# A hybrid decoder layer on one Trainium2 core: the first 128 tokens and the first 128 weight rows handled alone, the residual loaded in pieces

## Chip, core and metric

The kernel runs on one core of one Trainium2 chip. The metric is the device time of one execution in microseconds; three executions of the kernel before took 296.55, 297.00 and 297.28 us, so the median is 297.0 us. One further execution was profiled. All times inside it count from the start of its span.

## What is computed

One decoder layer over 512 tokens of width 1024, in f32:

```
h    = rms_norm(x, norm_w)                       # 512 x 1024
proj = h @ w_in                                  # 1024 x 4096, eight groups of 512 columns
hq, hf, hi, hg, aq, ak, av, ag = split(proj, 8)
o_h  = rms_norm(hgrn2(hq, hf, hi, lower_bound), hg_norm_w) * silu(hg)   # 4 heads, gated recurrence
o_a  = moba(rms(aq), rms(ak), av) * silu(ag)     # 8 heads, causal, blocks of 256 keys
out  = x + concat(o_h, o_a) @ w_out              # 1024 x 1024
```

## The kernel before

**Products.** Every product with a weight is made of three matmuls in the f32r format. Both factors are split in a high part (a cast) and a low part (the rest): the weights into `whi` (ScalarE, L109) and `wlo` (VectorE, one on GpSimd, L117), the turned and scaled x into `hTh` (ScalarE, L258) and `hTl` (VectorE, L266). One 128x512 result over 1024 rows takes 8 x 3 matmuls of 512 columns. The weights come in 40 tiles of 256 rows x 512 columns (512 KB); tile n is loaded by `load(n)`, cast by `split_hi(n)` and split by `split_lo(n)`. Group 0 (tiles 0 to 3) is the recurrent input, then seven more groups of the input projection, and 8 tiles of `w_out`.

**Turning x.** x is loaded in eight tiles: `x<i><h>` is 128 tokens (i = 0 to 3) by 512 columns (h = 0, 1), 256 KB. `x_turn(a, kp)` transposes two token tiles (a = 0: tokens 0 to 255; a = 1: 256 to 511) for the 256 columns of `kp`: four TensorE transposes into one PSUM tile, then two ScalarE evacuations of 256 columns that write `hTh`; `x_lo(a, kp)` writes `hTl` with two VectorE instructions.

**The opening.** The first stretch is written out by hand and all engines keep its order. The loads go to SP's queue in the order of `DSEQ`; the work follows the string `SEQ` (L128), word by word:

- `y7`: seven warm-up matmuls on a tile of ones (each is two instructions in the trace); `nt`: the norm weights are turned into a column;
- `t<a><kp>` and `l<a><kp>`: `x_turn` and `x_lo`; `wh<n>` and `wl<n>`: cast and split of weight tile n;
- `p<u><kp>`: for token tile u and weight tile kp the four matmuls that need only `whi`; `q<u><kp>`: the two with `wlo`;
- `sq<i>`: ScalarE's sum of squares of token tile i; `rs`: the root (VectorE, GpSimd); `rr`: the root as a row, copied over the partitions by DMA; `cv`, `cm`: small constants.

An engine works its words in this order and waits at the first one that is not ready. So TensorE's order is `y7 nt t00 t01 t10 t11 p00 q00 p10 q10 p30 q30 t03 p20 q20 t12 t02 p01 ...`, and ScalarE's is `t00 wh0 t01 sq0 t10 t11 wh1 t03 t12 t02 sq1 wh2 sq3 wh3 sq2 ...`. At the end of the string token tile by token tile gets its last products and `ev_i` evacuates it.

**The middle.** TensorE then runs through seven groups of 96 matmuls; the recurrence and the attention are threads whose steps a planner (`drive`, with the latencies in `LAT`) puts between these matmuls when the build expects their inputs to be ready. The planner's clock counts matmuls and transposes only.

**The output product.** `out_h` multiplies the recurrent half with the first four `w_out` tiles while the attention runs. Each of its eight results uses one of two PSUM tiles of the pool `pacc`. `out_fin` (L674 to L683) adds x to each result: at the first result of a column half it loads all four token tiles of x for this half in one DMA of 1 MB into `res` (L680), and VectorE adds the PSUM tile to it (L681). `res` lies in the buffer of `hTl`, so this load waits for the last matmul that reads `hTl`. `out_a` later adds the attention half and stores the result.

Of the kernel before, what the change touches and what calls it, by code (L numbers as in the profile page):

```python
# [8 lines left out]
F32 = mybir.dt.float32  # L9
F32R = mybir.dt.float32r  # L10
I32 = mybir.dt.int32
AF = mybir.ActivationFunctionType
ALU = mybir.AluOpType
# [8 lines left out]
def kernel(  # L22
# [12 lines left out]
    nc = tc.nc  # L35
    P = 128
    T, DM = x.shape[1], x.shape[2]
    NT = T // P
# [7 lines left out]
    xv = x[0].rearrange("(i p) c -> p i c", p=P)  # L46
# [4 lines left out]
    wpool = ctx.enter_context(tc.tile_pool(name="wpool", bufs=WB))  # L51
# [3 lines left out]
    ptr = ctx.enter_context(tc.tile_pool(name="ptr", bufs=2, space=bass.MemoryType.PSUM))  # L55
# [6 lines left out]
    xt = []  # L62
# [23 lines left out]
    W = {}  # L86
    raws = {}
    raw0 = []

    def load(n):  # L90
        if n < 0 or n >= len(stream):
            return
        src, c0, kp = stream[n]
        if n < WB:
            if n % 2 == 0:
                raw0.append(big.tile([P, 2, 2, 512], F32, tag=("f", "k", "q")[n // 2], name="raw0"))
            raw = raw0[n // 2][:, n % 2]
        else:
            raw = wpool.tile([P, 2, 512], F32, tag="raw", bufs=RB, name="raw")
        nc.sync.dma_start(  # L100
            out=raw,
            in_=src[kp * 256:(kp + 1) * 256, c0:c0 + 512].rearrange("(k p) c -> p k c", p=P))
        raws[n] = raw

    def split_hi(n):
# [15 lines left out]
    def split(n):  # L121
        if n < len(stream):
            split_hi(n)
            split_lo(n)

    POOL_LO = (3,)
    LAT = dict(lm=4.544, lev0=9.2567, lev=4.4882, copy=1.9908, rms=5.7036, silu=15.1764, qk=14.2881, soft=2.5598, softn=0.0041, acopy=4.5215, st=1.5748, ch=6.6909, DEPTH=2)
    SEQ = 'y7 nt t00 wh0 t01 sq0 t10 l00 t11 wl0 p00 q00 l01 wh1 p10 q10 l10 p30 q30 wl1 t03 l11 p20 q20 t12 t02 sq1 p01 q01 wh2 l03 l12 sq3 wh3 p21 q21 p11 q11 sq2 l02 p31 q31 wl2 p32 q32 rs wl3 p02 q02 p22 q22 cv t13 p12 q12 rr cm l13'  # L128
    DSEQ = 'x00 nw x10 w0 x20 x30 x01 x31 x11 w1 x21 w2 w4 v w3 w5'
    POOL_LO = (3,)  # L130
    for w in DSEQ.split():
        if w == "nw":
# [23 lines left out]
    hTh = big.tile([P, KT, T], F32R, tag="hTh", name="hTh")  # L156
    hTl = big.tile([P, KT, T], F32R, tag="hTl", name="hTl")
# [14 lines left out]
    def mm(o, a, b, start, stop, us):  # L172
        nc.tensor.matmul(o, a, b, start=start, stop=stop)  # L173
        clock[0] += us

    def tr(o, a):
        nc.tensor.transpose(o, a, ident)  # L177
        clock[0] += 0.109

    def spawn(gen, lat=0.0):  # L180
        threads.append([clock[0] + lat, (), gen, lat])
# [33 lines left out]
    X = {}  # L215
    rst = const.tile([P, NT], F32, name="rst")
    ssx = const.tile([P, NT], F32, name="ssx")
    nwc = const.tile([P, KT], F32, name="nwc")
# [29 lines left out]
    def x_turn(a, kp):  # L248
        wide = a == 0 and kp % 2 == 1
        tp = (psc if wide else ptr).tile([P, 512], F32, tag="sc" if wide else "tr", name="tp")  # L250
        X["tp", a, kp] = tp
        for d in range(2):
            kt = 2 * kp + d
            for i in range(2):
                tr(tp[:, (2 * d + i) * P:(2 * d + i + 1) * P], xt[2 * a + i][:, kt * P:(kt + 1) * P])
        for d in range(2):
            kt = 2 * kp + d
            nc.scalar.activation(hTh[:, kt, a * 256:a * 256 + 256], tp[:, d * 256:d * 256 + 256],  # L258
                                 AF.Copy, scale=nwc[:, kt:kt + 1])

    def x_lo(a, kp):
        tp = X["tp", a, kp]
        for d in range(2):
            kt = 2 * kp + d
            ts_ = slice(a * 256, a * 256 + 256)
            nc.vector.scalar_tensor_tensor(hTl[:, kt, ts_], tp[:, d * 256:d * 256 + 256], nwc[:, kt:kt + 1],  # L266
                                           hTh[:, kt, ts_].bitcast(F32), op0=ALU.mult, op1=ALU.subtract)


    def acc_tile(wide):  # L270
        return (psc if wide else pacc).tile([P, 512], F32, tag="sc" if wide else "acc", name="acc")
# [27 lines left out]
    k = big.tile([P, HH, T], F32, tag="k", name="k")  # L299

    def ev_i(u, ps):
        nc.scalar.activation(it[:, u, :], ps, AF.Copy, scale=rst[:, u:u + 1])
# [147 lines left out]
    def states():  # L450
        yield (LAT["st"], ("lev", 0), ("lev", 1))
        for n in range(NT - 1):
            cs = slice(n * P, (n + 1) * P)
            tp = ptr.tile([P, 512], F32, tag="tr", name="tp")
            for h in range(HH):
                tr(tp[:, h * P:(h + 1) * P], k[:, h, cs])
            kst = scratch()
            nc.scalar.copy(kst, tp)
            yield LAT["copy"]
            us = psc.tile([P, 512], F32, tag="sc", name="us")  # L460
            for h in range(HH):
                es = slice(h * DK, (h + 1) * DK)
                mm(us[:, es], kst[:, h * P:(h + 1) * P], it[:, n, es], True, True, 0.218)
            Sn = scratch()
            if n == 0:
                nc.vector.tensor_copy(Sn, us)
            else:
                for h in range(HH):
                    es = slice(h * DK, (h + 1) * DK)
                    m = (h % 2) * 4 + n  # L470
                    nc.vector.scalar_tensor_tensor(Sn[:, es], S[n][:, es], TL[h // 2][:, m:m + 1], us[:, es],
                                                   op0=ALU.mult, op1=ALU.add)
            S[n + 1] = Sn
            done[("S", n + 1)] = clock[0]
# [70 lines left out]
    A = {}  # L545
# [111 lines left out]
    res = {}  # L657
# [16 lines left out]
    def out_fin(part, hf, u, ps):  # L674
        cs = slice(hf * 512, hf * 512 + 512)
        if part == 0 and u == 0:
            if hf == 0:
                res["t"] = big.tile([P, 2, NT, 512], F32, tag="hTl", name="res")
            res[hf] = res["t"][:, hf]
            nc.sync.dma_start(out=res[hf], in_=xv[:, :, cs])  # L680
        nc.vector.tensor_tensor(res[hf][:, u, :], ps, res[hf][:, u, :], op=ALU.add)  # L681
        if part == 1:
            nc.sync.dma_start(out=ov[:, u, cs], in_=res[hf][:, u, :])  # L683
# [128 lines left out]
    with tc.manual_schedule(engines={mybir.EngineType.PE}):  # L812
        with tc.manual_schedule():
            accs = {}

            def part(u, kp, low):
                us = slice(u * P, (u + 1) * P)
                if u not in accs:
                    accs[u] = acc_tile(u >= 2)
                hi, lo = W[kp]  # L820
                for d in range(2):
                    kt = 2 * kp + d
                    wh, wl = hi[:, d, :], lo[:, d, :]
                    prods = ((hTh[:, kt, us], wl),) if low else ((hTh[:, kt, us], wh), (hTl[:, kt, us], wh))
                    for j, (a, b) in enumerate(prods):
                        mm(accs[u], a, b, kt == 0 and not low and j == 0, kt == KT - 1 and low, 0.216)

            def part_hi(u, kp):
                part(u, kp, False)

            def part_lo(u, kp):
                part(u, kp, True)

            acts = dict(cm=const_masks, cv=const_vec, sq=x_sq, rs=x_rstd, rr=x_rows, y=warm_up, nt=nw_col, t=x_turn, l=x_lo, p=part_hi, q=part_lo,
                        wh=split_hi, wl=split_lo)
            for w in SEQ.split():
                name = w.rstrip("0123456789")
                acts[name](*([int(w[1:])] if name == "y" else [int(ch) for ch in w[len(name):]]))
            for n in range(4, WB):
                split(n)  # L840
            for u in range(4):
                part_hi(u, 3)
                part_lo(u, 3)
                ev_i(u, accs[u])
            for kp in range(4):
                del W[kp]
                split(kp + WB)

        q2 = big.tile([P, 2, HH, T], F32, tag="q", name="q2")
        q = q2[:, 1]  # L850
        G = big.tile([P, NT, 512], F32, tag="G", name="G")
        gT = big.tile([P, NP, T], F32, tag="gT", name="gT")
        spawn(levels(0))
        spawn(levels(1))
        spawn(states())
        spawn(chunks())
        fa = fill_a()
        started = [False]

        def filler():  # L860
            yield from fa
            start_attention()
            wait_for(*[("read", n) for n in range(NT)])
            yield from out_h()

        drive(filler())
        for _ in out_a():
            pass
# [27 lines left out]
```

## Time and profile before

| | |
|---|---|
| three executions | 296.55, 297.00, 297.28 us |
| profiled execution | 297.17 us, of which the span between first and last instruction is 295.4 us |
| TensorE matmul busy | 287.6 us (97%) |
| VectorE, ScalarE, GpSimd busy | 175.0, 132.7, 57.1 us |
| DMA | 31.0 MB, 105 GB/s on average |

PE is TensorE's matmuls and transposes, PEld its weight loads, DVE VectorE, ACT ScalarE, POOL GpSimd, SP the engine that issues the DMAs. In a row of the timeline the first number is the start, the second the length (of the whole group, where it ends in a count such as x4), and what stands in brackets is the idle time just before it and what ended it. Matmuls overlap, so their lengths say less than the distance between their starts. In a row of a table by stretches the columns are: stretch, length, busy time of PE, PEld, DVE, ACT, POOL (with counts), granted TensorE clock, DMA share, GB/s.

### The profile page before, as it was taken

The page shows a single profiled execution, that of the slowest core. Times are in us where ns is not written, and L with a number is a line of the kernel's source. Part 1 is how long each engine was busy: PE and PEld are TensorE (multiplying, and loading weights), DVE is VectorE, ACT ScalarE, POOL GpSimd, SP SyncE. Part 2 cuts the span into 40 slices and gives each one's busy share as a digit, 9 for nine tenths or more (in the row PEclk, how much of TensorE's full clock was granted, in tenths as well). Part 3 has the DMA queues.
Part 4 walks back from the last instruction along what each step waited for, and adds up shares of the span by engine and source line. Part 5 has one row for each costly group of instructions (what it writes and reads, how often), then busy time and mean ns, then how long its engine had stood idle before and what let it go on. Part 6 is the DMA issues. An engine that isn't in the chain of part 4 may idle for free.

```text
span 295.4 us, 5115 instructions
## 1 busy us (share of the span) xinstructions
PE 287.6 (97%) x1945; PEld 236.7 (80%) x1945; DVE 175.0 (59%) x379; ACT 132.7 (45%) x248; POOL 57.1 (19%) x92
## 2 busy tenths in 40 slices
PE   7799999999999999999999999999999999999995
PEld 6588888888787777898888888888887787878884
DVE  3552653653699998357855785585384585653232
ACT  3754644420430475225511743753577676763000
POOL 1004201064000000010274223320004534330000
PEclk9999999999999999999999999999999999999999
DMA  6972375160260006100620099468287000000123
GB/s 189 352 282 104 15 106 201 43 242 0 73 213 4 2 2 227 60 0 0 215 73 0 8 261 208 95 168 207 47 229 279 0 2 0 2 2 2 71 101 112
DMA packets 21546, 31.00 MB, mean 105 GB/s; under 512 B 1413, under 2 KB 8338, under 8 KB 21522
## 3 DMA queue, kind: packets, MB, share of 16 engines
q1 hardware_dynamic: 21522, 30.68, 35.5%
q8 instruction: 15, 0.25, 0.3%
q14 instruction: 9, 0.07, 0.1%
HBM read 25.17 MB, written 2.10 MB: 92 GB/s over the span
## 4 chain that ended last, share of the span: by engine, by line
PE 93%; DMA 5%; SPq 1%; DVE 0%; issue 0%; DVEq 0%
PE acc L173 74%; PE tp L177 6%; PE ot L173 4%; PE sc L173 3%; PE pl L173 3%; DMA res<-in_x_dram 3%; DMA x<-in_x_dram 2%; PE ops L173 2%; PE us L173 1%; SPq L71 0%; DVE res L681 0%; SPq L100 0%; DVE res L717 0%; SPq L133 0%; PE tpv L778 0%
## 5 line engine op out<-in xcount | busy, mean ns | idle before, releaser
L173 PE MATMUL acc<-whi,hTh 128*128 128x512 f32 x160 | 65.3, 408 | 0.0
L173 PE MATMUL acc<-whi,hTl 128*128 128x512 f32 x160 | 63.0, 394 | 0.0
L173 PE MATMUL acc<-wlo,hTh 128*128 128x512 f32 x160 | 60.0, 391 | 0.0
L117 DVE TENSOR_TENSOR wlo<-raw,whi 128x1024 fp32r<-128x1024 f32 x39 | 47.1, 1230 | 12.1 <-ACT whi L109 11.6
L109 ACT CAST whi<-raw 128x1024 fp32r<-128x1024 f32 x40 | 41.5, 1048 | 13.4 <-DMA raw<-in_w_in_dram 6.3
L173 PE MATMUL acc<-hTh,whi 128*128 128x512 f32 x96 | 38.2, 397 | 0.0
L173 PE MATMUL acc<-hTh,wlo 128*128 128x512 f32 x96 | 37.5, 391 | 0.0
L173 PE MATMUL acc<-hTl,whi 128*128 128x512 f32 x96 | 37.4, 389 | 0.0
L163 POOL TENSOR_TENSOR r<-v,mh 128x8 f32<-128x8 f32 (+1 forms) x12 | 17.2, 1430 | 99.6 <-DVE v L161 99.5
L173 PEld LDWEIGHTS acc<-whi,hTl 128*128 128x128 f32 x160 | 30.3, 190 | 6.4
L173 PEld LDWEIGHTS acc<-whi,hTh 128*128 128x128 f32 x160 | 30.3, 190 | 6.3
L173 PEld LDWEIGHTS acc<-wlo,hTh 128*128 128x128 f32 x160 | 30.4, 190 | 5.9
L615 POOL TENSOR_SCALAR scr<-scr,rl 128x512 f32<-128x512 f32 (+3 forms) x32 | 17.0, 536 | 47.2 <-DVE rl L614 38.5
L173 PEld LDWEIGHTS acc<-hTh,wlo 128*128 128x128 f32 x96 | 18.0, 188 | 4.0 <-DVE wlo L117 0.2
L173 PEld LDWEIGHTS acc<-hTh,whi 128*128 128x128 f32 x96 | 18.0, 188 | 3.6
L173 PEld LDWEIGHTS acc<-hTl,whi 128*128 128x128 f32 x96 | 18.1, 188 | 3.5
L612 ACT ACTIVATE scr<-scr,nm 128x512 f32<-128x512 f32 (+3 forms) x32 | 17.7, 556 | 6.7 <-DVE nm L608 6.4
L173 PE MATMUL acc<-whi,mTa 128*128 128x512 f32 (+1 forms) x72 | 20.4, 367 | 0.0
L681 DVE TENSOR_TENSOR res<-acc,res 128x512 f32<-128x512 f32 x15 | 10.3, 689 | 15.7 <-PE acc L173 13.3
L177 PE MATMUL tp<-ident,scr 128*128 128x128 f32 x128 | 19.1, 275 | 0.0
L608 DVE CUSTOM_DVE_ANT_0 scr<-sc,bias 128x512 f32<-128x512 f32 (+3 forms) x32 | 14.6, 487 | 6.5 <-PE sc L173 6.2
L177 PEld LDWEIGHTS tp<-ident,scr 128*128 128x128 f32 x128 | 15.0, 140 | 4.0 <-issue 1.4
(138 smaller groups left out, 428.4 us busy)
## 6 DMA issues: line engine op xcount, KB each, us to landing
raw<-in_w_in_dram SPq DMA_DIRECT2D x32, 512.0 KB, 3.7
raw<-in_w_out_dram SPq DMA_DIRECT2D x8, 512.0 KB, 3.9
x<-in_x_dram SPq DMA_DIRECT2D x8, 256.0 KB, 6.4
res<-in_x_dram SPq DMA_DIRECT2D x2, 1024.0 KB, 9.1
out_dram<-res SPq DMA_DIRECT2D x7, 256.0 KB, 2.0
K<-K SPq DMA_DIRECT2D x8, 128.0 KB, 5.9
KL<-KL SPq DMA_DIRECT2D x8, 128.0 KB, 5.9
Q<-scr SPq DMA_DIRECT2D x8, 128.0 KB, 3.7
```

The source lines that it names most:

```text
L109: nc.scalar.copy(hi, raw)
L117: eng.tensor_sub(lo, raw, hi.bitcast(F32))
L163: nc.gpsimd.tensor_tensor(r, v, mh[:, 0:n], op=ALU.pow)
L173: nc.tensor.matmul(o, a, b, start=start, stop=stop)
L177: nc.tensor.transpose(o, a, ident)
L608: nc.vector.tensor_tensor_reduce(out=z[:, 0:n], in0=sc[:, 0:n], in1=bias[:, j, T - n:T], op0=ALU.add, op1=ALU.min, scale=1.0, scalar=3e38, ...
L612: nc.scalar.activation(z[:, 0:n], z[:, 0:n], AF.Exp, bias=nm, scale=-1.0, accum_out=l)
L615: nc.gpsimd.tensor_scalar(z[:, 0:n], z[:, 0:n], rl, 1.0, op0=ALU.mult, op1=ALU.mult)
L681: nc.vector.tensor_tensor(res[hf][:, u, :], ps, res[hf][:, u, :], op=ALU.add)
```

## The change

Three things are changed.

1. The first weight tile is loaded in two DMAs of 128 rows each, cast in two halves (`A0`, `B0`) and split in two halves (`a0`, `b0`). The order of the loads puts it ahead of x10, x20 and x30, and tile 1 ahead of the second column halves of x; tile 3 moves ahead of tile 4.
2. `t00`, the turn of tokens 0 to 255 for the first 256 columns, becomes `s00` and `s10`: one token tile each, two transposes, two evacuations of 128 columns (`x_turn1`), and their low parts `k00`, `k10` (`x_lo1`). The products of weight tile 0 become `P<u><kt>`: three matmuls for one token tile and 128 weight rows (`part1`). They are spread between the transposes, and the warm-up is cut in `y5` and `y3`. From `p32` on the string is the old one.
3. The residual is loaded in four DMAs of 256 KB per column half instead of one of 1 MB.

```diff
-        nc.sync.dma_start(
-            out=raw,
-            in_=src[kp * 256:(kp + 1) * 256, c0:c0 + 512].rearrange("(k p) c -> p k c", p=P))
+        rows = src[kp * 256:(kp + 1) * 256, c0:c0 + 512].rearrange("(k p) c -> p k c", p=P)
+        for ks in ((slice(0, 1), slice(1, 2)) if n == 0 else (slice(0, 2),)):
+            nc.sync.dma_start(out=raw[:, ks], in_=rows[:, ks])
...
-    SEQ = 'y7 nt t00 wh0 t01 sq0 t10 l00 t11 wl0 p00 q00 l01 wh1 p10 q10 l10 p30 q30 wl1 t03 l11 p20 q20 t12 t02 sq1 p01 q01 wh2 l03 l12 sq3 wh3 p21 q21 p11 q11 sq2 l02 p31 q31 wl2 p32 q32 rs wl3 p02 q02 p22 q22 cv t13 p12 q12 rr cm l13'
-    DSEQ = 'x00 nw x10 w0 x20 x30 x01 x31 x11 w1 x21 w2 w4 v w3 w5'
+    SEQ = 'y5 nt A0 y3 s00 a0 B0 k00 P00 b0 s10 P01 k10 P10 t10 P11 l10 wh1 t01 P20 P21 l01 wl1 t11 P30 P31 l11 p01 q01 sq0 t03 p11 q11 t12 t02 sq1 p21 q21 wh2 l03 l12 sq3 wh3 p31 q31 sq2 l02 wl2 p32 q32 rs wl3 p02 q02 p22 q22 cv t13 p12 q12 rr cm l13'
+    DSEQ = 'x00 nw w0 x10 x20 x30 w1 x01 x11 x31 x21 w2 w3 w4 v w5'
...
+    def x_turn1(i, kp):
+        tp = ptr.tile([P, 512], F32, tag="tr", name="tp")
+        X["tp1", i, kp] = tp
+        for d in range(2):
+            kt = 2 * kp + d
+            tr(tp[:, d * P:(d + 1) * P], xt[i][:, kt * P:(kt + 1) * P])
+        for d in range(2):
+            kt = 2 * kp + d
+            nc.scalar.activation(hTh[:, kt, i * P:(i + 1) * P], tp[:, d * P:(d + 1) * P],
+                                 AF.Copy, scale=nwc[:, kt:kt + 1])
...
-            nc.sync.dma_start(out=res[hf], in_=xv[:, :, cs])
+            for z in range(NT):
+                nc.sync.dma_start(out=res[hf][:, z, :], in_=xv[:, z, cs])
...
+            def part1(u, kt):
+                us = slice(u * P, (u + 1) * P)
+                if u not in accs:
+                    accs[u] = acc_tile(u >= 2)
+                hi, lo = W[kt // 2]
+                wh, wl = hi[:, kt % 2, :], lo[:, kt % 2, :]
+                for j, (a, b) in enumerate(((hTh[:, kt, us], wh), (hTh[:, kt, us], wl), (hTl[:, kt, us], wh))):
+                    mm(accs[u], a, b, kt == 0 and j == 0, False, 0.216)
+
+            def half_hi(d):
+                if d == 0:
+                    W[0] = tuple(wpool.tile([P, 2, 512], F32R, tag=t, name=t) for t in ("whi", "wlo"))
+                nc.scalar.copy(W[0][0][:, d], raws[0][:, d])
+
+            def half_lo(d):
+                hi, lo = W[0]
+                nc.vector.tensor_sub(lo[:, d], raws[0][:, d], hi[:, d].bitcast(F32))
```

## Rows read from the trace of the kernel before

**Rows 1.** Part 4 of the page: shares of the span, by engine, of the chain that ended last.

```profile
PE 93%; DMA 5%; SPq 1%; DVE 0%; issue 0%; DVEq 0%
```

**Rows 2.** The same chain in order of time: start, length, what. The pieces in it that are not TensorE's, and what follows the second.

```profile
2.96 6.96 DMA x<-in_x_dram
...
217.23 8.04 DMA res<-in_x_dram
225.36 0.70 DVE res L681
226.11 3.02 PE acc L173 x12
```

**Rows 3.** Timeline of PE in the opening: warm-up, transposes (tp), products (acc). The last two are the start of `p32` and of `q32`.

```profile
1.04 3.36 PE L241 MATMUL wp<-scr 128*128 128x128 f32 x14 [1.04 <-DVE warm L151]
5.63 1.76 PE L177 MATMUL tp<-ident,x 128*128 128x128 f32 x7 [0.63 <-DMA x<-in_x_dram]
...
8.96 0.45 PE L177 MATMUL tp<-ident,x 128*128 128x128 f32 x1 [1.57 <-DMA x<-in_x_dram]
9.96 1.75 PE L177 MATMUL tp<-ident,x 128*128 128x128 f32 x7 [0.55 <-DMA x<-in_x_dram]
11.36 0.77 PE L173 MATMUL acc<-whi,hTh 128*128 128x512 f32 x1
...
12.36 0.63 PE L173 MATMUL acc<-whi,hTh 128*128 128x512 f32 x1
12.79 0.63 PE L173 MATMUL acc<-whi,hTl 128*128 128x512 f32 x1
...
13.85 0.40 PE L173 MATMUL acc<-whi,hTh 128*128 128x512 f32 x1
...
18.43 1.03 PE L177 MATMUL tp<-ident,x 128*128 128x128 f32 x8
...
24.79 0.39 PE L173 MATMUL acc<-whi,hTh 128*128 128x512 f32 x1
...
25.69 0.61 PE L173 MATMUL acc<-wlo,hTh 128*128 128x512 f32 x2
```

**Rows 4.** Timeline of SP's queue in the opening: start and length of the issue of the loads.

```profile
8.03 1.20 SPq L100 DMA_DIRECT2D raw<-in_w_in_dram  x2
9.93 0.28 SPq L74 DMA_DIRECT2D vec<-in_hg_lb_logits_dram  x1
10.72 0.25 SPq L75 DMA_DIRECT2D vec<-in_hg_norm_w_dram  x1
11.40 0.22 SPq L77 DMA_DIRECT2D vec<-in_q_norm_w_dram  x1
12.08 0.22 SPq L78 DMA_DIRECT2D vec<-in_k_norm_w_dram  x1
13.44 0.22 SPq L77 DMA_DIRECT2D vec<-in_q_norm_w_dram  x1
```

**Rows 5.** Timeline of ACT: the cast of weight tile 0 and the first sum of squares, with what they waited for; `t12` and `t02`; `sq1`; `wh2`; two casts in a row.

```profile
8.03 1.04 ACT L109 CAST whi<-raw 128x1024 fp32r<-128x1024 f32 x1 [0.62 <-DMA raw<-in_w_in_dram]
...
10.79 1.06 ACT L223 ACTIVATE sq<-x 128x1024 f32<-128x1024 f32 x1 [0.97 <-DMA x<-in_x_dram]
...
19.06 1.57 ACT L258 ACTIVATE hTh<-tp,nwc 128x256 fp32r<-128x256 f32 x4 [0.98 <-PE tp L177]
20.51 1.07 ACT L223 ACTIVATE sq<-x 128x1024 f32<-128x1024 f32 x1
...
21.55 1.06 ACT L109 CAST whi<-raw 128x1024 fp32r<-128x1024 f32 x1
...
30.69 1.99 ACT L109 CAST whi<-raw 128x1024 fp32r<-128x1024 f32 x2
```

**Rows 6.** Timeline of DVE: two `x_lo` in a row and two splits in a row.

```profile
19.94 1.66 DVE L266 SCALAR_TENSOR_TENSOR hTl<-tp,nwc,hTh 128x256 fp32r<-128x256 f32 x4 [0.94 <-ACT hTh L258]
...
32.29 2.34 DVE L117 TENSOR_TENSOR wlo<-raw,whi 128x1024 fp32r<-128x1024 f32 x2
```

**Rows 7.** Timelines around the residual: SP's issues, VectorE's first addition, TensorE's first product after its wait.

```profile
214.05 3.09 SPq L100 DMA_DIRECT2D raw<-in_w_out_dram  x3
217.23 1.07 SPq L680 DMA_DIRECT2D res<-in_x_dram  x2
...
225.36 0.69 DVE L681 TENSOR_TENSOR res<-acc,res 128x512 f32<-128x512 f32 x1 [2.21 <-DMA res<-in_x_dram]
...
226.11 0.50 PE L173 MATMUL acc<-whi,mThh 128*128 128x512 f32 x1 [0.70 <-DVE res L681]
```

**Rows 8.** Busy time by stretches (columns as said above).

```profile
10.00:14.00 4.00, 4.00 (x14) 3.49 (x15) 2.00 (x5) 3.17 (x7) 0.00 (x0) 1.00 1.06 405
...
80.00:120.00 40.00, 40.00 (x617) 31.42 (x616) 37.48 (x71) 15.80 (x32) 0.00 (x0) 1.00 0.30 104
...
214.00:222.00 8.00, 8.00 (x38) 6.71 (x37) 6.28 (x14) 5.97 (x10) 0.65 (x1) 1.00 0.83 236
222.00:224.00 2.00, 2.00 (x16) 1.80 (x15) 0.33 (x2) 1.68 (x6) 1.87 (x4) 1.00 1.05 400
```

**Rows 9.** Timelines of POOL (the split of tile 3) and of PE (the first product that reads it, `wlo` of tile 3).

```profile
27.00 2.38 POOL L117 TENSOR_TENSOR wlo<-raw,whi 128x1024 fp32r<-128x1024 f32 x1
...
32.03 0.62 PE L173 MATMUL acc<-wlo,hTh 128*128 128x512 f32 x2
```

More of the change, by code (lines that the diff above doesn't have):

```diff
@@ L259, in x_turn, with x_lo1 @@
                                  AF.Copy, scale=nwc[:, kt:kt + 1])
+    def x_turn1(i, kp):
[8 more added lines that the diff above has]
+                                 AF.Copy, scale=nwc[:, kt:kt + 1])
+    def x_lo1(i, kp):
+        tp = X["tp1", i, kp]
+        for d in range(2):
+            kt = 2 * kp + d
+            ts_ = slice(i * P, (i + 1) * P)
+            nc.vector.scalar_tensor_tensor(hTl[:, kt, ts_], tp[:, d * P:(d + 1) * P], nwc[:, kt:kt + 1],
+                                           hTh[:, kt, ts_].bitcast(F32), op0=ALU.mult, op1=ALU.subtract)
     def x_lo(a, kp):
@@ L834 @@
             acts = dict(cm=const_masks, cv=const_vec, sq=x_sq, rs=x_rstd, rr=x_rows, y=warm_up, nt=nw_col, t=x_turn, l=x_lo, p=part_hi, q=part_lo,
-                        wh=split_hi, wl=split_lo)
+                        wh=split_hi, wl=split_lo, s=x_turn1, k=x_lo1, P=part1,
+                        A=half_hi, B=lambda _: half_hi(1), a=half_lo, b=lambda _: half_lo(1))
             for w in SEQ.split():
```

## The prediction, made before the result was known

> **What bounds the kernel now.** I read the chain that ended last first: 93% of it is TensorE [rows 1]. So the useful number of matmuls, which the change leaves alone, sets the time, and something is to be had only where TensorE stands still or runs slowly. The chain in order of time then shows two such places: 6.96 us behind the loads of x at the start, and 8.04 us in which the load of the residual stands in the chain, with an addition of 0.70 us behind it [rows 2]. The change touches both.
>
> The timeline of PE in the opening is to show three things [rows 3]. The first product starts at 11.36, after idle times that loads of x ended (0.63, 1.57 and 0.55 us). Products start 0.43 us apart (12.36, 12.79): 512 columns in 0.43 us is the 1.2 GHz level. From 24.79 to 25.69 four take 0.90 us, 0.23 us each, which is 2.4 GHz; the step lies just ahead of 13.85. The granted clock says 1.00 throughout this stretch [rows 8], so here the spacing tells the level, not that column. Ahead of the step PE had been without a pause since 9.96.
>
> **When the loads land.** SP starts load number n+8 when number n has landed: number 11 starts at 8.03, when the cast of weight tile 0 (number 3) starts [rows 4, 5]; number 13 at 9.93 is x30, which PE takes at 9.96 [rows 3, 4]; number 14 at 10.72 is x01, which ScalarE squares at 10.79 [rows 4, 5]. By that x10 lands at 5.6, w0 8.0, x20 8.9, x30 9.9, x01 10.7, x31 11.4, x11 12.1, w1 13.4. Landing follows the order of issue, so I put the new order on the same curve of bytes: w0's first half at 5.6 (x10's place), its second 6.8 (halfway to 8.0), x10 8.0, x20 8.9 and x30 9.9 as before, w1 11.4, all x by 14.1. Nothing later than w1 comes near a deadline.
>
> **The opening, step by step.** Durations of instructions that stand in a row behind one another: evacuation of a pair of 256 columns 0.73 (four in 1.57, then the sum of squares at 20.51), cast 0.94 (two in 1.99, one in 1.05), sum of squares 1.04 [rows 5]; `x_lo` 0.83, split 1.11 [rows 6]. Per 128 columns that is 0.095 on ScalarE (0.94 against 0.37 for 768 columns less) and 0.12 on VectorE, so the halves cost: cast 0.56, evacuations 0.54, split 0.64, `k` 0.60. None of them stands in the trace. As bounds I take half of the whole and the whole; between these the first products move by about 0.5 us either way. Each result is usable 0.1 us after its slot, and PE's transposes reach ScalarE 0.17 us after the next could start.
>
> `s00` is through on PE at 5.7 (warm-up 0.24 per instruction, transposes 0.22 [rows 3]). ScalarE has `A0` ahead of it, until 6.2, then the evacuations until 6.7. `P00` starts at 6.8 instead of 11.36, and its third product waits for `a0` and `k00` (VectorE to 7.74) and ends at 8.3. x10 has landed by then. At 0.43 each, `s10` ends at 8.8, `P01` at 10.0.
>
> The clock comes next. PE now runs nearly without pause from 6.8, 3.2 us before the 9.96 of the old order. I move the step by the same 3.2 us, from 13.4 to 10.2. Bounds: 8.4 (as soon as the gaps of `P00` end) and 13.4 (no earlier than before). The Trainium skill ("TensorE: Matmul & The Clock Gate", Part 1) says that this moment differs from run to run of one kernel, because what watches the activity doesn't start with the kernel; one profiled run cannot show it, and by that rule every moment between these bounds has to be allowed for.
>
> With 10.2: `P10` ends at 10.9, `t10` (x30 is there at 9.9) 11.4, `P11` 12.1, `t01` 12.5. `P20` waits 0.4 us for `l10` (evacuation to 12.4, VectorE 0.83) and ends at 13.6. Then 0.23 per product and 0.115 per transpose: `P21` 14.3, `t11`, `P30`, `P31` 16.1, `p01`, `q01` 17.5, `t03` 17.9, `p11`, `q11` 19.3, `t12` 19.8, `t02` 20.2, twelve products 22.96.
>
> Here a new wait appears. In the old order 24 products stand between `t02` and `p32`, now 12. ScalarE still has two pairs of evacuations, `sq1` and `wh2` between: 19.77 + 0.17 + 0.73 + 0.73 + 1.04 + 0.94 + 0.1 = 23.5. `p32` therefore waits 0.56 us; four products end at 24.4; `wlo` of tile 2 is ready at 23.5 + 1.11 + 0.15 = 24.8, so `q32` waits another 0.34 and starts at 24.77. Before it started at 25.69 [rows 3]; counted the same way the old order gives 25.7. The gain of the opening is 0.92 us. With the clock at 8.4 it is 1.4, at 13.4 it is -0.1. Behind the waiting `p32` and `q32` PE has only the old order, which the threads take up unchanged. What is late next is `wlo` of tile 3 on POOL: ready 2.65 us before its product (29.38 against 32.03 [rows 9]). After the change the cast of tile 2 ends 0.9 us later than before (23.5 against 22.6 [rows 5]) and this split with it, while the product comes 0.92 earlier: 0.8 us are left. It doesn't bind.
>
> That the gain reaches the end: the planner's clock counts the same matmuls and transposes, so PE's order behind stays. Where VectorE is nearly full (37.5 of 40 us, with PE at 40 of 40 [rows 8]) it works on evacuations that come earlier with PE.
>
> **The additional DMA issues** (one for w0, six for the residual) cost SP some 0.3 to 0.6 us each by the neighbouring rows [rows 4, 7]. They lie beside transfers: at 217 three weight tiles are still on their way, and no load but the residual stands behind them on SP.
>
> **The residual.** From 214 to 222 the core moved 8 x 236 GB/s = 1.89 MB [rows 8]; 1.57 MB of it are the three weight tiles issued just ahead [rows 7]. So at 222 the first 0.26 MB piece is through, and at 400 GB/s [rows 8] one more follows each 0.66 us. The whole half is through at about 223.8 and was seen as landed at 225.36, 1.5 us later; the first piece would then count at about 223.3, and its addition (0.69) end at 224.0. PE needs that PSUM tile at 225.41 (226.11 less 0.70 [rows 7]). The wait of 0.70 us goes. Bounds: nothing (the pieces land together) and 0.75. What is late next is the second piece, half a microsecond behind the first, and VectorE, which stood 2.21 us and gets its attention work done earlier. The Trainium skill ("DMA: Bandwidth & Descriptors", Rules for kernel authors) asks for at least 1 MiB per DMA; here x31 and x11, of 256 KB, land 0.68 us apart and w1, of 512 KB, 1.36 us after x11 [rows 4], the same 385 GB/s, so in a full queue the trace does not bear the rule out. By it each piece would come later, and the residual would give nothing.
>
> **Sum.** 0.92 + 0.70 = 1.62 us. The profiled execution took 297.17 us, a span of 295.4 and 1.8 around it; it becomes 295.55, span 293.8. It stands 0.17 above the median of 297.0, so the median becomes 295.4.
>
> **Rivals.**
> - *The clock steps no earlier* (13.4): the opening gives nothing, every product until then pays 0.20 us and only fills the former wait; the residual remains: 296.3. For it: pauses at 7.3 to 7.9 and the half-speed transposes between the products; against it: PE's pauses are shorter than before. The same time results if a later stage swallows the opening's gain; [rows 8] speak against that.
> - *The pieces land no earlier*: the opening alone, 296.1. Against it: loads land in order of issue.
> - *Slower: the halves of w0 are slow.* w0 took 2.4 us for 512 KB (5.6 to 8.0), the slowest load of the opening. If each half took as long as the whole did, w0's halves land at 6.8 and 9.2, x10 at 10.4 and all others 2.3 us later. The same steps (`P00` from 8.0, wait for x10 from 9.3 to 10.4, clock step later by the 0.44 us that 10.4 is behind 9.96) put `q32` at 27.5, 1.8 us late; less 0.70 that is +1.1: 298.1. It decides for slower when the loads behind w0 come about 2 us late; from 1 us on the opening gives nothing. Against it: the same bytes are in the queue, and 256 KB pieces cost no more elsewhere.
>
> **Chances.** Forecast 0.60, clock or loss later 0.22, pieces 0.10, slow halves 0.08. About 0.3% (0.9 us) is what a measurement of this kernel can tell from no change: faster means under 296.1. The forecast's own spread (0.92 between 0.4 and 1.4) keeps nearly all of it faster, 0.56, and half of the pieces' case and a little of the clock's add 0.08: faster 0.64, same 0.27, slower 0.09. Range: down to 297.0 - 1.4 - 0.75 less 0.6 for the opening's unmeasured halves and the spread of the times (0.7 over three), 294.2; up to 297.0, which takes in both mild rivals.
>
> **What would show it.** First product near 6.8 and products 0.23 us apart from about 10; an idle PE ahead of `p32`, ended by ScalarE's cast of tile 2, and ahead of `q32`, ended by VectorE; `q32` at 24.8; no idle PE at 225, and the first addition no later than 224 on the new scale. The prediction is wrong if products keep 0.43 us beyond 12, if x10 lands after 9, or if more than 0.3 us of PE's idle time appears between 32 and 215.

## The result, and the profile after

The changed kernel took 300.34 us (median of four executions, 299.82 to 301.13) against 297.14 for the kernel before beside it: a ratio of 1.013, 95% interval 1.008 to 1.018. Run once more in a later batch it took 299.00 against 296.66: 1.008, interval 1.005 to 1.011. So the change made the kernel about 1% slower; 295.4 was forecast. A ratio here and below is estimated from the single executions, without those more than 1.5% above the fastest of the same kernel, so it is not the quotient of the two medians. The profiled execution took 300.61 us, with a span of 298.8 against 295.4. The difference of 3.4 us lies in the two places that the change touches.

**The opening loses 2.3 us.** Timeline of PE in the kernel after, the rows that answer to [rows 3]; the last three are the start of `p32`, the start of `q32` and the turn of the root of the norm (`rp`), which started at 30.99 before and now starts at 33.30.

```profile
5.12 0.45 PE L177 MATMUL tp<-ident,x 128*128 128x128 f32 x2
7.34 0.50 PE L173 MATMUL acc<-whi,hTh 128*128 128x512 f32 x1 [1.78 <-ACT hTh L269]
7.80 0.50 PE L173 MATMUL acc<-wlo,hTh 128*128 128x512 f32 x1
9.80 0.79 PE L173 MATMUL acc<-whi,hTl 128*128 128x512 f32 x1 [1.49 <-DVE hTl L277]
10.39 0.63 PE L177 MATMUL tp<-ident,x 128*128 128x128 f32 x2
...
12.10 0.63 PE L173 MATMUL acc<-whi,hTh 128*128 128x512 f32 x1
12.52 0.63 PE L173 MATMUL acc<-wlo,hTh 128*128 128x512 f32 x1
...
14.65 0.63 PE L173 MATMUL acc<-wlo,hTh 128*128 128x512 f32 x1
...
26.60 0.50 PE L173 MATMUL acc<-whi,hTh 128*128 128x512 f32 x1 [0.45 <-ACT whi L109]
...
27.86 0.73 PE L173 MATMUL acc<-wlo,hTh 128*128 128x512 f32 x2
...
33.30 0.27 PE L232 MATMUL rp<-ident,rst 128*4 128x128 f32 x1
```

The first product comes four microseconds earlier than before, at 7.34. Then two things go wrong. The third product of `P00` waits 1.49 us for the low part of x, `hTl`. And from this product on they are 0.43 us apart until 15, where the old order was at 0.23 from 13.85. The same in the table by stretches, where the third number from the right is the granted clock:

```profile
7.00:8.00 1.00, 0.66 (x2) 0.37 (x2) 0.94 (x5) 1.00 (x4) 0.00 (x0) 1.00 0.89 344
8.00:9.00 1.00, 0.30 (x1) 0.00 (x0) 1.00 (x13) 0.06 (x1) 0.00 (x0) 0.83 1.05 365
9.00:10.00 1.00, 0.20 (x1) 0.20 (x1) 0.96 (x7) 0.00 (x0) 0.00 (x0) 0.50 0.99 309
...
14.00:15.00 1.00, 1.00 (x5) 0.89 (x4) 0.00 (x0) 0.53 (x2) 0.00 (x0) 0.50 1.05 399
15.00:16.00 1.00, 1.00 (x7) 0.71 (x6) 0.66 (x2) 1.00 (x2) 0.00 (x0) 0.75 0.79 290
```

Here the column tells the level too: 0.50 of 2.4 GHz is 1.2 GHz, from 9 to 15. It also tells that the clock had been up before: 0.83 between 8 and 9 means that it fell near 8.7, in the wait behind the second product. The lengths agree: two transposes at 5.12 took 0.45 us and two at 10.39 took 0.63; the first product behind a pause took 0.50 at 7.34 and 0.79 at 9.80. So the opening did not stay at the low level; it was at the high one when `P00` began and lost it in its pauses. VectorE's timeline says what `hTl` stood behind:

```profile
7.06 0.69 DVE L864 TENSOR_TENSOR wlo<-raw,whi 128x512 fp32r<-128x512 f32 x1 [3.11 <-ACT whi L860]
7.67 0.18 DVE L768 TENSOR_TENSOR gt<-ccol,s 128x32 int32<-128x32 int32 x1
...
9.30 0.18 DVE L783 TENSOR_SCALAR lmask<-part 128x32 int32<-128x32 int32 x1
9.40 0.60 DVE L277 SCALAR_TENSOR_TENSOR hTl<-tp,nwc,hTh 128x128 fp32r<-128x128 f32 x2
```

From 7.67 to 9.48 VectorE makes the masks of the recurrence (`const_tri`, L757 to L783), which nobody needs yet. They are no word of the string, and the build places them; that all engines keep the order of the opening holds for its words alone. In the old kernel they filled VectorE's idle time from 4.7 to 6.5, as the first and the last of those placed there show in its timeline:

```profile
4.72 0.18 DVE L748 TENSOR_TENSOR gt<-ccol,s 128x32 int32<-128x32 int32 x1
...
6.35 0.18 DVE L763 TENSOR_SCALAR lmask<-part 128x32 int32<-128x32 int32 x1
```

Now they stand between `a0` and `k00`.

**The middle** moves as one piece. The residual's load was issued at 217.23 [rows 7] and is issued at 219.49 now, 2.26 us later.

**The residual loses another 1.1 us.** Timelines of SP, VectorE, GpSimd and TensorE in the kernel after, answering to [rows 7]:

```profile
219.49 6.11 SPq L700 DMA_DIRECT2D res<-in_x_dram  x8
...
224.01 0.16 DVE L633 RECIPROCAL rl<-l 128x1 f32<-128x1 f32 x1 [0.54 <-ACT scr L631]
226.74 0.69 DVE L701 TENSOR_TENSOR res<-acc,res 128x512 f32<-128x512 f32 x1 [2.57 <-DMA res<-in_x_dram]
227.35 0.21 DVE L633 RECIPROCAL rl<-l 128x1 f32<-128x1 f32 x2
...
227.60 1.15 POOL L634 TENSOR_SCALAR scr<-scr,rl 128x384 f32<-128x384 f32 x2 [2.56 <-DVE rl L633]
...
228.24 1.11 PE L177 MATMUL tp<-ident,scr 128*128 128x128 f32 x6 [1.84 <-POOL scr L634]
```

Before, VectorE had four reciprocals of the attention (`rl`) and then the first addition; the last two of the four in the timeline of the kernel before:

```profile
222.39 0.16 DVE L614 RECIPROCAL rl<-l 128x1 f32<-128x1 f32 x1 [0.44 <-ACT scr L612]
222.99 0.16 DVE L614 RECIPROCAL rl<-l 128x1 f32<-128x1 f32 x1 [0.43 <-ACT scr L612]
```

Now it has two reciprocals, the addition, and the other two. The addition waits 2.57 us for its piece of x, and the reciprocals behind it, GpSimd's scaling and TensorE's transposes wait with it: 1.84 us of idle TensorE in place of the 0.70 of before [rows 7]. The first piece counted as landed 7.25 us after its issue, the whole half before 8.13 after.

### The profile page after: what moved, and what is told of

The parts are those of the page before. It is cut to its first block, busy times and chain, and to the rows that moved or that the text cites. A ratio compares the mean times of both kernels' runs of the same rounds, so it can differ in the third digit from the quotient of the medians.

```text
span 298.8 us, 5138 instructions
## 1 busy us (share of the span) xinstructions
PE 288.8 (97%) x1947; PEld 236.7 (79%) x1947; DVE 176.8 (59%) x382; ACT 132.9 (44%) x251; POOL 57.0 (19%) x92
## 4 chain that ended last, share of the span: by engine, by line
PE 91%; DMA 4%; DVE 2%; ACT 1%; issue 0%; SPq 0%; POOL 0%; ACTq 0%; DVEq 0%
PE acc L173 72%; PE tp L177 7%; PE ot L173 3%; PE sc L173 3%; PE pl L173 3%; DMA res<-in_x_dram 2%; PE ops L173 2%; DMA raw<-in_w_in_dram 2%; PE us L173 1%; DVE wlo L117 0%; ACT sq L223 0%; ACT hTh L258 0%; ACT whi L109 0%; DVE wlo L864 0%; ACT whi L860 0%
## 5 line engine op out<-in xcount | busy, mean ns | idle before, releaser
L173 PE MATMUL acc<-whi,hTh 128*128 128x512 f32 x160 | 66.1, 413 | 2.2 <-ACT hTh L269 1.8
L173 PE MATMUL acc<-wlo,hTh 128*128 128x512 f32 x160 | 61.4, 396 | 0.1
L117 DVE TENSOR_TENSOR wlo<-raw,whi 128x1024 fp32r<-128x1024 f32 x38 | 45.7, 1226 | 8.9 <-ACT whi L109 8.4
L109 ACT CAST whi<-raw 128x1024 fp32r<-128x1024 f32 x39 | 40.5, 1048 | 14.1 <-DMA raw<-in_w_in_dram 6.9
```

The source lines that it names most:

```text
L109: nc.scalar.copy(hi, raw)
L117: eng.tensor_sub(lo, raw, hi.bitcast(F32))
```

## Experiments

Twelve runs in three batches, each batch beside the kernel before; the last four ran on another chip than the first eight, so runs of different batches are compared by their ratios. Four theories stood at first: A, the masks ahead of `k00` cost the opening its gain; B, the finer order itself is slow, by the low clock; C, the pieces cost time because an addition got ahead of two reciprocals; D, the pieces cost nothing. All medians first, then what each says. Each run has twelve executions, the changed kernel again seven. The ratio is that to the kernel before in the same batch.

| run | median us (range) | before | ratio, 95% interval |
|---|---|---|---|
| changed, masks early | 298.49 (297.23 to 300.47) | 297.08 | 1.0043, 1.0013 to 1.0074 |
| changed, one load | 298.05 (296.39 to 298.95) | 297.08 | 1.0037, 1.0011 to 1.0063 |
| before, with pieces | 296.97 (295.65 to 299.12) | 297.08 | 1.0023, 0.9992 to 1.0054 |
| masks early, one load | 297.39 (296.16 to 298.34) | 297.08 | 1.0025, 0.9998 to 1.0051 |
| changed, again | 299.00 (298.14 to 301.22) | 296.66 | 1.0082, 1.0050 to 1.0114 |
| masks early, one load, cast first | 297.45 (296.11 to 297.74) | 296.66 | 1.0012, 0.9988 to 1.0037 |
| the same, pause filled | 295.40 (294.98 to 295.79) | 296.66 | 0.9966, 0.9947 to 0.9984 |
| masks early, pieces reversed | 296.94 (296.00 to 297.77) | 296.66 | 1.0007, 0.9985 to 1.0029 |
| before, pause filled | 295.33 (294.18 to 296.80) | 296.21 | 0.9976, 0.9951 to 1.0000 |
| masks early, reversed, filled | 294.97 (294.78 to 295.62) | 296.21 | 0.9956, 0.9932 to 0.9980 |
| changed, pause filled | 296.53 (295.70 to 298.52) | 296.21 | 1.0007, 0.9980 to 1.0033 |
| all four | 294.66 (294.47 to 295.00) | 296.21 | 0.9946, 0.9925 to 0.9967 |

**Masks early.** `const_tri` becomes a word of the string (`ct`), right behind `nt`.

```diff
-y5 nt A0 y3 s00 a0 B0 k00 P00
+y5 nt ct A0 y3 s00 a0 B0 k00 P00
```

> The changed kernel, with the 21 mask instructions of const_tri written into the opening's order right behind nt, where VectorE is idle, instead of being put by the build behind a0 and ahead of k00. Theory A (the loss of the opening comes from these instructions standing ahead of k00): k00 starts near 7.8 instead of 9.4, the third product of P00 near 8.4 instead of 9.8, the clock step comes as much earlier (about 14), and the time falls by 1.4 us to about 298.9. Theory B (the finer order itself is slow: halves, few products between waits, a low clock): P00 starts earlier, but PE waits elsewhere before the clock step, and the time stays within 0.5 us of the changed kernel's 300.3.

298.49: A, in part. The third product of `P00` starts at 8.48 instead of 9.80, `rp` at 30.84 instead of 33.30; the rest of these 2.46 us comes with the clock, which rose again at 11.7 in this execution and at 15.5 in the one above. By the ratios to before (1.0043 against 1.0082) this is worth 0.39%, 1.2 us, but the two intervals overlap, and the pair with one load in the same batch (298.05 and 297.39) gives 0.7. Nor are the masks out of the way. Written out as one word they run from 3.86 to 7.39 and now hold up `a0`, which the second product needs. Its timelines of VectorE and TensorE:

```profile
7.21 0.18 DVE L783 TENSOR_SCALAR lmask<-part 128x32 int32<-128x32 int32 x1
7.30 0.69 DVE L863 TENSOR_TENSOR wlo<-raw,whi 128x512 fp32r<-128x512 f32 x1
...
8.05 0.64 PE L173 MATMUL acc<-wlo,hTh 128*128 128x512 f32 x1 [1.18 <-DVE wlo L863]
```

In all seven profiles with the masks early this product starts at 8.05 or 8.06. No run has the masks behind `k00`. The residual stays bad, and this profile shows what an idle TensorE costs there beyond its own length. Its timeline of PE, then its table by stretches:

```profile
226.14 1.47 PE L177 MATMUL tp<-ident,scr 128*128 128x128 f32 x6 [2.18 <-POOL scr L634]
```

```profile
226.00:228.00 2.00, 1.85 (x10) 1.61 (x10) 1.10 (x8) 1.52 (x6) 1.13 (x4) 0.68 0.54 206
228.00:230.00 2.00, 2.00 (x7) 1.61 (x7) 0.89 (x6) 1.23 (x5) 1.53 (x4) 0.50 0.08 23
230.00:232.00 2.00, 2.00 (x11) 1.62 (x10) 0.00 (x0) 0.00 (x0) 0.93 (x2) 0.97 0.00 0
```

Behind a pause of 2.18 us TensorE was granted half its clock from about 226.7 to 230. The profiles of the pieces alone (2.41 us) and of the changed kernel again (2.35) show the same fall; in the execution above, with 1.84 us, the granted clock stayed at 1.00.

**One load per half of the residual.**

```diff
-            for z in range(NT):
-                nc.sync.dma_start(out=res[hf][:, z, :], in_=xv[:, z, cs])
+            nc.sync.dma_start(out=res[hf], in_=xv[:, :, cs])
```

> The changed kernel with the residual in one load per column half, as before. Theory C (the pieces made the build put the first addition ahead of two reciprocals on VectorE, and GpSimd and TensorE wait behind it): the four reciprocals stand ahead of the addition again, PE's idle time there is 0.7 us instead of 1.84, the time falls by 1.1 us to about 299.2. Theory D (the pieces cost nothing or help a little, the whole loss lies in the opening): the time stays at 300.3 or rises by up to 0.7.

298.05: C. By the ratios (1.0037 against 1.0082) it is worth 0.45%, 1.3 us, where 1.1 was expected, though these intervals too overlap a little. VectorE has its four reciprocals first again, and TensorE's idle time there is 0.27 us.

**The pieces alone, on the kernel before.**

```diff
-            nc.sync.dma_start(out=res[hf], in_=xv[:, :, cs])
+            for z in range(NT):
+                nc.sync.dma_start(out=res[hf][:, z, :], in_=xv[:, z, cs])
```

> The kernel before with the residual in pieces and nothing else changed. Theory C: the addition stands ahead of two reciprocals here too, PE is idle 1.8 us near 225, the time is 1.1 us above that of before, about 298.2. Theory D: no change, or up to 0.7 us faster.

Undecided: the median, 296.97, is D's number, but the interval of the ratio (0.9992 to 1.0054) takes in C's 1.1 us (0.37%) as well. Its profile, taken of its slowest execution (299.12), has C's turned order and 2.41 us of idle TensorE. The same profile shows something else: the opening is that of the kernel before, instruction for instruction, and yet its first product starts at 10.36 instead of 11.36 (the loads of x landed sooner), products come 0.23 us apart from 11.7 on instead of 13.4, and `rp` starts at 29.54 instead of 30.99. A single execution can differ by 1.5 us in the opening alone.

**Masks early and one load.** Both edits together.

> Both repairs: masks early and the residual in one load; what is left of the change is the new opening. Theories A and C: 300.3 - 1.4 - 1.1 = 297.8, within 1 us of before. Theory B with C: about 299.2. If the opening as I forecast it were right apart from the masks, it would be 0.9 us under before, 296.2.

297.39, close to A with C. So the two mechanisms bring the time back to about that of before, but they don't say why the gain of 0.92 that the prediction saw in the opening is missing. Its profile has `P00` at 7.14, an idle TensorE of 1.90 us ahead of it, products 0.43 us apart until 11.4, and 0.45 us of waiting at `p32`. The next batch took these one by one.

**The changed kernel again.**

> The changed kernel once more, unchanged, beside the three others of this batch. If the two mechanisms seen in its trace (the masks ahead of the low part of x in the opening, an addition ahead of two reciprocals at the residual) are built in, it is as slow as before: 299.5 to 300.8, and its profile again has a third product of P00 after 9 us and an idle PE over 1.5 us near 228. If the loss was the state of single executions, it comes out under 298.5.

299.00, between the two; the ratio's interval (1.0050 to 1.0114) says that a loss is built in, with a spread of 3 us between executions. Its profile has the same waits (1.49 us ahead of the third product, 2.35 us at the residual), but another clock: the third product (at 8.94, 0.50 long) was still at the high level, and the low one lasted from 9.4 to 12.8 instead of 8.7 to 15.5, with `rp` at 31.53.

**The cast first.** On masks early and one load, `wh2` ahead of `sq1`, which is what `p32` and `q32` waited for.

```diff
-t12 t02 sq1 p21 q21 wh2 l03
+t12 t02 wh2 sq1 p21 q21 l03
```

> Masks early, one load of the residual (297.4 before), and now the cast of weight tile 2 (wh2) ahead of the sum of squares of token tile 1 (sq1). Theory that the new wait at p32 and q32 (0.45 and some 0.3 us, ended by ScalarE's cast and VectorE's split) is on the path to the end: both waits go, 296.7. Rival, the time gained in the opening is taken up by a later wait or lost in the spread of the clock's step: unchanged, 297.4.

Nearer the rival by the median, 297.45; the ratio (1.0012 against 1.0025) lies between the two, inside its interval. The wait at `p32` is gone from the timeline, and `rp` starts 1.0 us earlier than without it (29.80 against 30.83); but the residual's load is issued only 0.2 us earlier. Where this goes is shown with the last run.

**The pause filled.** On top of that, four warm-up matmuls between `s00` and `P00`.

```diff
-s00 a0 B0 k00 P00
+s00 y4 a0 B0 k00 P00
```

> As the run with the cast first, and four more warm-up matmuls between the two transposes of s00 and the products P00, where TensorE stood idle for 1 to 1.9 us. Theory that the clock's step comes a fixed way after TensorE has become busy without a pause: the step comes near 9.5 instead of 11.4, some five products cost 0.43 - 0.23 = 0.20 us less each, 1.0 us in all: 295.7. Rival, what TensorE does in that pause doesn't move the step: as the run with the cast first (296.7), or up to 0.3 us more, where the added matmuls stand ahead of P00.

The theory of the clock: 295.40, 2.05 us less than the run without them by the medians and 1.4 by the ratios, where 1.0 was expected. Timeline of PE in its opening:

```profile
5.37 1.06 PE L241 MATMUL wp<-scr 128*128 128x128 f32 x8
6.46 0.50 PE L173 MATMUL acc<-whi,hTh 128*128 128x512 f32 x1
8.05 0.50 PE L173 MATMUL acc<-wlo,hTh 128*128 128x512 f32 x1 [1.08 <-DVE wlo L862]
...
9.51 0.39 PE L173 MATMUL acc<-whi,hTl 128*128 128x512 f32 x1
9.73 0.40 PE L173 MATMUL acc<-whi,hTh 128*128 128x512 f32 x1
9.97 0.40 PE L173 MATMUL acc<-wlo,hTh 128*128 128x512 f32 x1
```

From the first products on the distance is that of 2.4 GHz (9.51, 9.73, 9.97), although TensorE still stands 1.08 us behind the first, for the masks. The eight warm-up instructions took 1.06 us, where the ten at the start of the program took 2.51: the clock was up by then, and it did not fall again. 1.3 of the 2.05 us are in the opening (`rp` at 28.48 against 29.80). The rest belongs to the residual, whose load landed sooner in this execution, so that TensorE stood 0.35 us there against 1.27.

**The pieces in reverse.** On masks early: four loads as in the change, but the first addition needs the one issued last, and the build leaves it behind the four reciprocals.

```diff
-            for z in range(NT):
+            for z in reversed(range(NT)):
```

> Masks early and the residual in four pieces, issued in reverse order, so that the first addition needs the piece issued last. VectorE then has all four reciprocals ahead of the first addition, as with one load. Theory that the pieces cost time only because the build, which expects the first piece early, puts the addition ahead of two reciprocals: as masks early with one load, 297.4 (up to 298 if the eight loads on the queue land the last piece late). Rival, four loads on the queue cost the time by themselves: as masks early with the pieces in order, 298.5.

C: 296.94 against 298.49 in order (by the ratios 0.36%, 1.1 us). Four loads cost nothing that shows in the time; what costs is VectorE's order. Its timeline of VectorE, with no idle time of TensorE around it:

```profile
223.68 0.17 DVE L633 RECIPROCAL rl<-l 128x1 f32<-128x1 f32 x1 [0.43 <-ACT scr L631]
225.26 1.29 DVE L701 TENSOR_TENSOR res<-acc,res 128x512 f32<-128x512 f32 x2 [1.42 <-PE tp L177]
```

What ended VectorE's idle time ahead of the addition is TensorE in this profile, not a load. In the two later runs with reversed pieces it is a load (1.30 and 1.27 us), and TensorE doesn't wait there either.

**The kernel before with its pause filled**, as a control: is it the finer order or the clock that gains?

```diff
-t00 wh0 t01 sq0 t10 l00
+t00 wh0 t01 y5 sq0 t10 l00
```

> The kernel before, with five warm-up matmuls between t01 and t10, where TensorE stood 1.57 us for the load of x20; nothing else. Theory that idle stretches in the opening hold TensorE at the lower clock: the step comes near the first product (11.4) instead of 13.4, some five products cost 0.20 us less each: 295.7. Rival, only the finer order of the changed kernel can use it: 296.7 as before, or up to 0.5 us more where the added matmuls stand ahead of a transpose that is ready.

295.33, a ratio of 0.9976: the theory's number, with an interval that just reaches 1. Its products are 0.23 us apart from the first at 10.73, although the loads still keep TensorE idle for 1.92 and 0.37 us behind the added matmuls. So the clock can be had without the finer order.

**Pieces reversed and pause filled**, without the cast first.

> As the run with masks early and the pieces reversed (296.9), and the four warm-up matmuls in the pause ahead of P00, without the change to the cast's order. Theory of the clock: products 0.23 us apart from the first on, 1.3 us less: 295.6, and executions within 1 us of each other. Rival, the gain of the run with the pause filled came from the cast's order after all: 296.9.

294.97, below the theory's 295.6, and twelve executions within 0.84 us. Against the kernel before with its pause filled (ratios 0.9956 and 0.9976) the repaired finer order is 0.2% ahead, with intervals that overlap.

**The changed kernel with only its pause filled.**

> The changed kernel with only the four warm-up matmuls in the pause ahead of P00; masks and pieces as in the change. Theory of the clock alone: the low level cost the changed kernel most of the opening, the third product still waits until about 9.6 for the masks but all from there are 0.23 us apart, rp at 30.0 to 30.5 instead of 33.3; the residual loses its 1 us as before: 296.5 to 297. Rival, the pause behind the second product (1.5 us, by the masks) takes the clock down again: 298.5 to 299.5.

296.53: the theory. The same three lines of PE as shown for the kernel after, in this run:

```profile
6.82 0.48 PE L173 MATMUL acc<-whi,hTh 128*128 128x512 f32 x1
7.14 0.40 PE L173 MATMUL acc<-wlo,hTh 128*128 128x512 f32 x1
8.95 0.50 PE L173 MATMUL acc<-whi,hTl 128*128 128x512 f32 x1 [1.41 <-DVE hTl L277]
...
10.37 0.40 PE L173 MATMUL acc<-whi,hTh 128*128 128x512 f32 x1
10.60 0.40 PE L173 MATMUL acc<-wlo,hTh 128*128 128x512 f32 x1
```

The masks' wait is there as before (1.41), and all products run at 2.4 GHz; `rp` starts at 30.13. Against the changed kernel (1.0082 to 1.0007) four warm-up matmuls in idle time give back 0.75%, 2.2 us: by these estimates the largest single part of the loss. Of the twelve executions one has a mean granted clock of 0.994, the others 0.998 or more, and it is the slowest (298.52). With the clock up, the masks early are worth less than before: `rp` at 29.54 in the run above against 30.13 here, 0.6 us.

**All four**: masks early, pieces reversed, pause filled, cast first.

> As the run with the pieces reversed and the pause filled, and the cast of weight tile 2 ahead of the sum of squares. If p32's wait is on the path, 0.5 us less than that run, 295.1; rival, what is gained there is lost in a wait for the turned x behind it (0.25 us in the profile with the cast first) and at the residual: the same within 0.3 us, 295.6.

294.66, 0.54% under the kernel before (interval 0.33 to 0.75%), the best of all, within 0.53 us over twelve executions. Between the theory (-0.5) and the rival (the same): -0.3. `rp` starts 1.06 us earlier than without the cast first (28.48 against 29.54), but the residual's load is issued only 0.20 us earlier. The timelines of POOL, DVE and PE in this run show where most of the 0.86 us went:

```profile
27.16 2.40 POOL L117 TENSOR_TENSOR wlo<-raw,whi 128x1024 fp32r<-128x1024 f32 x1
...
27.17 2.41 DVE L805 TENSOR_TENSOR ldf<-col,lmx 128x4 f32<-128x4 f32 x1
...
29.61 0.72 PE L173 MATMUL acc<-wlo,hTh 128*128 128x512 f32 x2
...
31.68 0.85 DVE L285 SCALAR_TENSOR_TENSOR hTl<-tp,nwc,hTh 128x256 fp32r<-128x256 f32 x2
...
32.20 0.50 PE L173 MATMUL acc<-whi,hTl 128*128 128x512 f32 x1 [0.24 <-DVE hTl L285]
```

A subtraction of 128x4 takes 2.41 us, as long as GpSimd's split of weight tile 3 beside it; the small steps behind it and the last low part of x (`l13`) follow, for which TensorE then waits. The split itself ends at 29.56, and the product that reads it starts right behind, at 29.61; this takes back 0.2 us, and `l13` some 0.5. Without the cast first the same subtraction starts at 28.22, takes 1.34 and ends at the same time, 29.6. So an opening that is earlier than this meets a chain that starts with the split on GpSimd, and gains no more.

## Why the prediction was wrong

Its sum was -0.92 in the opening and -0.70 at the residual. The first became about +2.3, the second +1.1 in the profiled execution. What failed is the order on VectorE in both places, and the clock. Step by step:

1. *"its third product waits for `a0` and `k00` (VectorE to 7.74) and ends at 8.3"* Wrong. It started at 9.80, because the masks, 1.8 us of VectorE's time, stood ahead of `k00`. The prediction followed VectorE by the words of the string and forgot the work that isn't in it and that the build can put anywhere. In the old trace these instructions lie in the idle time from 4.7 to 6.5; the question "will they stay there?" was never asked. Putting them early was worth 0.4 to 1.2 us, depending on the pair of runs, and only moved their wait from the third product to the second.
2. *"I move the step by the same 3.2 us, from 13.4 to 10.2", with "no earlier than before" as the late bound.* Wrong, and the largest error. The prediction knew one rise of the clock, which follows from when TensorE's steady work begins, and no fall. In the profile it was up when `P00` began, fell near 8.7 and rose again at 15.5, outside the bounds. The sentence "PE now runs nearly without pause from 6.8" held neither for the pause ahead of `P00` (0.60 to 1.90 us in the profiles, by when the first half of w0 landed, 4.9 to 6.4) nor for the one behind its first or second product. Of seven profiles of the changed opening without the added matmuls, five show this fall, between 8.0 and 9.4; in the other two (one load; pieces reversed) products were at the low level from the first and the rise came at 13.5 and 13.1. With the pause filled it fell in none of the five openings, the control on the old order included. In the changed kernel this was worth 2.2 us. The rival "the clock steps no earlier" took 13.4 as the worst case and so priced it at 0.9 us above the forecast; that cheap work in a pause would keep the clock was no term of the sum.
3. *`p32` and `q32`.* Right in kind and size: 0.56 and 0.34 forecast, 0.45 and some 0.23 in the profile, ended by the cast and the split as said.
4. *"What is late next is `wlo` of tile 3 on POOL ... it doesn't bind."* Right for the change: the split ended at 33.33 and its product started at 34.34, 1.0 us later, where 0.8 was forecast. With the opening 4.8 us earlier, in the last run, it binds, by itself (0.2 us) and by holding up VectorE's small subtraction and with it `l13` (some 0.5), which took back most of the 1.06 us that the cast first gained.
5. *"the first piece would then count at about 223.3, and its addition (0.69) end at 224.0"; "The wait of 0.70 us goes."* Wrong in both halves. The addition started at 226.74; on the old scale, 2.26 us less, 224.48 instead of 223.3: the piece came 0.9 us sooner than the whole half, not 2.1. And the order on VectorE was taken as fixed: an addition that the build can expect early was put ahead of two reciprocals that were ready earlier. With the order restored and four loads kept (pieces reversed) the wait is gone, as forecast.
6. *The middle.* Right: 2.31 us late at `rp`, 2.26 at the issue of the residual's load.
7. The rival on the slower side, slow halves of w0, was the wrong mechanism, though the direction came out as it said. The halves were as quick as forecast or nearly (4.9 to 6.4 against 5.6).

Still open: what the pieces alone cost the kernel before, whose median shows nothing while its one profile shows the turned order and its wait. That the wait changes with the moment at which the residual lands is a guess that no run tested. Open too is why the clock rises during the warm-up in some executions and not in others. And the worths given for masks, pieces and pause don't add up: together they are more than the loss, because the masks' wait is one of the pauses in or behind which the clock fell.

## What to carry to other kernels

A hand-written order fixes only what it names: before moving work, list every instruction on the same engines that the build may place, and write into the order those that must not come between. A wait that is put on an in-order engine is paid by everything behind it, so an addition whose input comes by DMA belongs behind the reciprocals that are ready. And when the start of TensorE's work is moved forward, count the pauses that this opens between the warm-up and the steady work: here the clock, once up, fell again in or right behind them, and cheap matmuls in the first pause were worth more than the finer order.

## What the runs showed of the hardware that was not expected

**The level of the clock in the opening is a property of one execution.** In the profile of the kernel before the clock rose only at 13.4, 2.0 us behind the first product. In that of the same opening with the pieces alone, eight transposes at 4.53 took 1.24 us, where seven took 1.76 before; the granted clock then fell near 8.3, right behind a pause of 2.42 us, and rose at 11.7, 1.3 us behind the first product. The Trainium skill ("TensorE: Matmul & The Clock Gate", Part 1) says that the moment of the rise changes from run to run of one kernel; the trace agrees, though 1.0 of these 1.7 us came with an earlier first product. Of the 35 executions of the kernel before in the last batch, the 14 with a mean granted clock of 0.994 took 295.2 to 296.2 us, and the 18 with 0.998 or 1.00 took 294.4 to 298.0, all but two of them over 296.2. Where the pause is filled and the masks are early, the spread goes with it: twelve executions of each such run lie within 0.53 to 0.84 us, those 35 within 5.2 us (294.36 to 299.57).

**The column of the granted clock doesn't always show the low level.** In the kernel before it says 1.00 while products are 0.43 us apart; in the kernel after it says 0.50 at the same distance. In every profile here it says 1.00 over the first four microseconds, where the warm-up's matmuls of 128 columns come 0.21 us apart (0.11 behind the rise, in the first run with the pause filled). So 1.00 ahead of the first change in the column says nothing, and a mean of 1.00 can belong to the slower execution. The distance tells the level in both.

**A 128x4 subtraction on VectorE took 2.41 us** beside a split on GpSimd, 1.34 where it came later, and 0.16 in the kernel before, where it started after the split had ended (29.67 against 29.38). The Trainium skill ("SBUF — State Buffer", SBUF: two separate sides) says that VectorE with two inputs from SBUF and GpSimd reading SBUF share a pair of ports, and that the later one stands still until the other is through; the trace agrees, as the first two ended with the split (29.6 in both) and the third lay behind it. The changed kernel itself has it too: 1.37 us, up to the split's end at 33.3.
